# Mixing the scan's output: where the norm's scale and shift, the bonus and the mean are applied

## The chip, the core and the metric

The kernel runs on one core of a Trainium2 chip. The metric is the device time of one execution in microseconds (us). The core has a matrix engine (TensorE, "PE", with its weight loads "PEld"), three engines for elementwise work (VectorE, "DVE"; ScalarE, "ACT"; GpSimd, "POOL") and a queue that issues DMAs (SyncE, "SP"). Each engine works through its own instructions in a fixed order and waits, instruction by instruction, on what other engines have finished.

## The reference, cut to what matters

One layer of a diffusion trunk: 256 context and 1024 latent tokens of 1024 channels go through a normalised input projection, a gated convolution group and a two-direction recurrent scan (RWKV-7, eight heads of 64), an output projection with residual, and a gated MLP with a 3x3 convolution. What the change touches is the end of the scan: the sum `y` of both directions is normalised per head, scaled and shifted, a bonus is added, and the result is gated.

```python
def rwkv_output(y, r, k, v, g_lo, lp):
    mu = jnp.mean(y, axis=-1, keepdims=True)
    var = jnp.mean(jnp.square(y - mu), axis=-1, keepdims=True)
    yn = ((y - mu) * lax.rsqrt(var + GN_EPS)).reshape(bsz, t, D_RWKV) * lp["ln_g"] + lp["ln_b"]
    bonus = jnp.sum(to_heads(r) * to_heads(k) * lp["r_k"], axis=-1, keepdims=True) * to_heads(v)
    gate = jax.nn.sigmoid(g_lo) @ lp["g_up"]
    return (yn + bonus.reshape(bsz, t, D_RWKV)) * gate
```

## The kernel before

Tokens are tiled by 128, so the latents are eight tiles, t = 0 to 7. The program's stages follow one another: norm and input projection (to about 500 us of the span), decays and small inversions, the scan (about 690 to 898 us), the output side of the mixer, and the MLP: its up product (`pf`, L1105) with the 3x3 convolution, and its down product (`pf`, L1185), which fill PE from about 961 us to the end.

The scan runs in rounds, and each round takes one chunk of 64 tokens in either direction (`steps`). Its chain on PE is `ry` (L753, L761), a copy of `ry` to `rh` (L763: on ACT for one direction, on DVE for the other), `pu` (L773), a negated copy to `vu` (L777 on ACT, L779 on DVE), `ps` (L785) with the state's update on DVE (L788), and `ry` again (L794). POOL scales the chunk's `car` tile (L651) and adds up the two directions' output (L811).

From the round in which both directions have met, tiles become complete two at a time: 3 and 4, 2 and 5, 1 and 6, 0 and 7. The table `TAIL` says in which round a tile's stages are put in: `m` is `mix`, `o` is `outp` (the output projection, PE `po`, L907, 24 matmuls a tile, then DVE L1001), `h` is `to_h2` (transposes L1021 and the scaled copies L1029, L1031, L1033, L1034 that make the MLP's input). These stages are generators, and `fill` takes some steps of them between the parts of a round. Below this, a list scheduler sets the order of the instructions on every engine, so an edit in `mix` moves its neighbours too.

`mix` for one tile, by line: L965 sums `y` over each head, L966 multiplies the 8 sums by 1/64, L967 takes the mean off (all DVE); L970 squares on ACT; L972 sums the squares; `rstd_of` makes 1/sqrt(var) (L163, ACT L169, L171 to L175); L975 multiplies by it (DVE). Then POOL multiplies by the norm's scale (L976) and adds its shift (L977), and multiplies the values `vt` by the bonus factor (L978). L980 (DVE) adds `vt`, L983 (DVE) multiplies by the gate `pg` (PE, L982), L987 transposes on PE (`py`), and L989 (ACT) and L990 (DVE) split the result into the two parts `chl` that `outp` multiplies by. `mix_load` issues the DMAs of `vt` and the gate's input.

Of the kernel before, what the change touches and what calls it, by code (L numbers as in the profile page):

```python
# [11 lines left out]
ALU = mybir.AluOpType  # L12
# [75 lines left out]
def hybrid_kernel(  # L88
# [7 lines left out]
    V, A, G, PE, SY = nc.vector, nc.scalar, nc.gpsimd, nc.tensor, nc.sync  # L96
# [64 lines left out]
    def rstd_of(pool, ss, n, scale, eps):  # L161
        v = pool.tile([128, n], F32, name="rvar", bufs=2)
        V.tensor_scalar(out=v, in0=ss, scalar1=scale, scalar2=eps, op0=ALU.mult, op1=ALU.add)  # L163
        return newton(pool, v, n)
# [17 lines left out]
    bon = cp.tile([128, 8, 8], F32, name="bon")  # L182
# [23 lines left out]
    with ExitStack() as s2:  # L206
# [106 lines left out]
        while n_ < NT:  # L313
# [4 lines left out]
                               in1=prm[:, P_N1:P_N1 + 8].unsqueeze(2).to_broadcast([128, 8, 2]), op0=ALU.add, op1=ALU.mult)  # L318
# [636 lines left out]
    def mix(t):  # L955

        y, vt, sgt = mixin[t]
        xt = op.tile([128, D], F32, name="xt", bufs=XT)
        if t not in X2:
            SY.dma_start(xt, x2d[t])  # L960
        hl = op.tile([128, 2, 4, 128], F32R, name="chl", bufs=NH)
        y3 = y.rearrange("p (h n) -> p h n", n=64)
        v3 = vt.rearrange("p (h n) -> p h n", n=64)
        mu = op.tile([128, 8], F32, name="mu", bufs=2)
        V.tensor_reduce(out=mu, in_=y3, axis=mybir.AxisListType.X, op=ALU.add)  # L965
        V.tensor_scalar(out=mu, in0=mu, scalar1=1.0 / 64, scalar2=None, op0=ALU.mult)  # L966
        V.tensor_tensor(out=y3, in0=y3, in1=mu.unsqueeze(2).to_broadcast([128, 8, 64]), op=ALU.subtract)  # L967
        yield
        sq = op.tile([128, 8, 64], F32, name="ysq", bufs=2)
        A.activation(sq, y3, AF.Square)  # L970
        vr = op.tile([128, 8], F32, name="vr", bufs=2)
        V.tensor_reduce(out=vr, in_=sq, axis=mybir.AxisListType.X, op=ALU.add)  # L972
        rs = rstd_of(op, vr, 8, 1.0 / 64, epsg)
        yield
        V.tensor_tensor(out=y3, in0=y3, in1=rs.unsqueeze(2).to_broadcast([128, 8, 64]), op=ALU.mult)  # L975
        G.tensor_tensor(out=y, in0=y, in1=lng[:, 0, :], op=ALU.mult)  # L976
        G.tensor_tensor(out=y, in0=y, in1=lng[:, 1, :], op=ALU.add)  # L977
        G.tensor_tensor(out=v3, in0=v3, in1=bon[:, t, :].unsqueeze(2).to_broadcast([128, 8, 64]), op=ALU.mult)  # L978
        yield
        V.tensor_tensor(out=y, in0=y, in1=vt, op=ALU.add)  # L980
        pg = pp.tile([128, 512], F32, name="pg", tag="px", bufs=2)
        PE.matmul(pg, sgt, gup, start=True, stop=True)  # L982
        V.tensor_tensor(out=y, in0=pg, in1=y, op=ALU.mult)  # L983
        yield
        py = pp.tile([128, 4, 128], F32, name="py", tag="px", bufs=2)
        for j in range(4):
            PE.transpose(py[:, j, :], y[:, 128 * j:128 * j + 128], ident)  # L987
        yield
        A.copy(hl[:, 0], py)  # L989
        V.tensor_tensor(out=hl[:, 1], in0=py, in1=hl[:, 0].bitcast(F32), op=ALU.subtract)  # L990
        tiles[t] = [xt, hl]
# [45 lines left out]
    TPOS = {t: (0, 128 * (t - 2)) if 2 <= t < 6 else (1, 128 * (t if t < 2 else t - 4)) for t in range(8)}  # L1037

    stages = {"m": mix, "o": outp, "h": to_h2}
    ppc = Banks(ry=B2[0], pu=B2[1])  # L1040
    w_raw(0)
# [14 lines left out]
    for r in range(16):  # L1056
# [3 lines left out]
        if r == RC:  # L1060
            fill(999)
            sa.close()
            op = so.enter_context(tc.tile_pool(name="op", bufs=1, side="left", reuse_waits="tile"))
            lng = op.tile([128, 2, 512], F32, name="lng")
# [66 lines left out]
    for f in (1, 0, *range(2, NF)):  # L1131
# [24 lines left out]
        for hf, c0, n, t0 in PIECES:  # L1156
            V.tensor_tensor(out=act[:, t0:t0 + n], in0=pv[hf][:, c0:c0 + n],  # L1157
                            in1=acc.rearrange("p r c -> p (r c)")[:, t0:t0 + n], op=ALU.mult)
# [29 lines left out]
    for th in range(2):  # L1188
# [8 lines left out]
        for q in range(4):  # L1197
# [3 lines left out]
            t = 4 * th + q  # L1201
# [50 lines left out]
```

## Time and profile before

| what | value |
|---|---|
| median of 3 runs | 1689.11 us (1687.71 to 1690.62) |
| the profiled execution | 1681.7 us, its span 1679.9 us |
| mean granted TensorE clock in it | 0.949 |
| busy, share of the span | PE 91%, PEld 74%, DVE 69%, ACT 37%, POOL 34% |
| span of the mixing, from its first DVE operation to its last | 791.5 to 946.2 us |

Times in views of the trace are microseconds from the span's start. A row of the timeline gives the start, the duration, engine, line, operation and tiles of an instruction, and in brackets how long its engine had been idle before it and what ended that. A tile's name stands without its number.

### The profile page before, as it was taken

To read this page: it belongs to the slowest core of one execution; us is meant where nothing else is said; L and a number is where in the kernel's file an instruction comes from. 1 tells how busy PE (TensorE), PEld (TensorE's weight loads), DVE (VectorE), ACT (ScalarE), POOL (GpSimd) and SP (SyncE) were. 2 spreads that over 40 slices of the span, in tenths; PEclk is the share of its full clock that TensorE was granted. 3 is DMA by queue.
4 is the path that set the end of the run, shared out by engine and by line. 5 is a ranking of instruction groups with operands and counts; after the bars stand their busy time and mean duration, and the time that the engine had idled before them with its cause. 6 is when DMAs were issued, how large, how long until landed. Compare 5 with 4: busy or idle time off the path is not lost.

```text
span 1679.9 us, 27373 instructions
## 1 busy us (share of the span) xinstructions
PE 1534.4 (91%) x10567; PEld 1240.1 (74%) x10567; DVE 1154.1 (69%) x1783; ACT 619.9 (37%) x1158; POOL 567.3 (34%) x498
## 2 busy tenths in 40 slices
PE   7699999989898876898788899999999999999997
PEld 2588678767776766787666678888888887788886
DVE  5964526899899987445677678777777777346645
ACT  2654325535545235443454322221112112325323
POOL 2454413433233222412545232222222222545643
PEclk9699999989998867999899999999999999999999
DMA  9396556556665685989643112111111111533531
GB/s 322 110 290 203 173 169 189 170 164 212 209 198 167 219 261 177 335 262 278 187 133 116 51 50 62 41 49 51 50 51 51 51 40 48 190 101 124 175 93 59
DMA packets 233171, 246.93 MB, mean 147 GB/s; under 512 B 18496, under 2 KB 171685, under 8 KB 233041
## 3 DMA queue, kind: packets, MB, share of 16 engines
q1 hardware_dynamic: 232624, 245.02, 46.9%
q8 instruction: 84, 1.38, 0.4%
q14 instruction: 47, 0.38, 0.1%
q0 software_dynamic: 416, 0.16, 0.0%
HBM read 178.79 MB, written 66.33 MB: 146 GB/s over the span
## 4 chain that ended last, share of the span: by engine, by line
PE 51%; DVE 13%; ACT 2%; DMA 2%; issue 2%; POOL 1%; SPq 0%; DVEq 0%; ACTq 0%; POOLq 0%
PE pf L1105 26%; PE pf L1185 13%; PE po L907 2%; PE pco L907 2%; DVE acc L1152 2%; PE pj L355 2%; DVE ti L673 2%; PE ry L761 2%; DVE tmp L671 1%; PE ps L785 1%; PE pu L773 1%; DMA car<-ar_dram 1%; PE ry L753 1%; DVE S L788 1%; PE ry L794 1%
## 5 line engine op out<-in xcount | busy, mean ns | idle before, releaser
L1105 PE MATMUL pf<-h,fhi 128*128 128x512 f32 x1408 | 385.6, 391 | 7.6 <-DVE act L1157 4.1
L1105 PEld LDWEIGHTS pf<-h,fhi 128*128 128x128 f32 x1408 | 265.2, 189 | 64.3 <-DVE act L1157 4.5
L355 PE MATMUL pj<-hx,whi 128*128 128x512 f32 (+1 forms) x976 | 299.7, 385 | 3.0 <-DVE hx L329 1.9
L1152 DVE SCALAR_TENSOR_TENSOR acc<-gp,prm,acc 128x1024 f32<-128x1024 f32 x176 | 272.9, 1552 | 6.0
L106 POOL TENSOR_TENSOR flo<-fraw,fhi 128x1024 fp32r<-128x1024 f32 x50 | 123.2, 2465 | 305.9 <-ACT fhi L105 305.9
L1105 PE MATMUL pf<-h,flo 128*128 128x512 f32 x704 | 224.3, 391 | 0.0
L355 PEld LDWEIGHTS pj<-hx,whi 128*128 128x128 f32 x976 | 180.8, 192 | 39.6 <-issue 3.9
L355 PE MATMUL pj<-hx,wlo 128*128 128x512 f32 (+1 forms) x488 | 187.0, 383 | 0.0
L1185 PE MATMUL pf<-dhi,ahl 128*128 128x512 f32 x640 | 163.1, 389 | 0.3 <-DVE ahl L1177 0.3
L1177 DVE TENSOR_TENSOR ahl<-act,ahl 128x512 fp32r<-128x512 f32 x44 | 86.2, 1970 | 100.1 <-ACT ahl L1176 100.1
L1105 PEld LDWEIGHTS pf<-h,flo 128*128 128x128 f32 x704 | 132.7, 189 | 27.8 <-POOL flo L106 0.2
L105 ACT CAST fhi<-fraw 128x1024 fp32r<-128x1024 f32 x50 | 52.7, 1054 | 267.7 <-issue 162.5
L1185 PEld LDWEIGHTS pf<-dhi,ahl 128*128 128x128 f32 x640 | 120.0, 188 | 25.6 <-DVE ahl L1177 0.8
L106 POOL TENSOR_TENSOR dlo<-fraw,dhi 128x1024 fp32r<-128x1024 f32 x40 | 98.5, 2466 | 92.2 <-ACT dhi L105 91.4
L106 POOL TENSOR_TENSOR wlo<-wraw,whi 128x1024 fp32r<-128x1024 f32 x26 | 64.4, 2477 | 132.9 <-ACT whi L105 131.9
L1150 DVE TENSOR_SCALAR acc<-gp,prm 128x1024 f32<-128x1024 f32 x22 | 42.5, 1932 | 97.2 <-ACT gp L1142 97.2
L355 PEld LDWEIGHTS pj<-hx,wlo 128*128 128x128 f32 x488 | 93.6, 192 | 16.9 <-issue 0.8
L1185 PE MATMUL pf<-dlo,ahl 128*128 128x512 f32 x320 | 89.1, 389 | 0.0
L651 POOL TENSOR_TENSOR car<-car,pcs 128x512 f32<-128x512 f32 (+1 forms) x38 | 39.6, 1055 | 140.8 <-DMA car<-ar_dram 114.7
L105 ACT CAST dhi<-fraw 128x1024 fp32r<-128x1024 f32 x40 | 41.9, 1050 | 105.0 <-PE pf L1185 87.5
L602 PE MATMUL px<-arO,kbO 64*128 64x128 f32 (+1 forms) x640 | 65.5, 308 | 13.2 <-DVE xrO L606 8.9
L602 PEld LDWEIGHTS px<-arO,kbO 64*128 64x128 f32 x640 | 52.5, 205 | 31.4 <-issue 23.2
(292 smaller groups left out, 2620.1 us busy)
## 6 DMA issues: line engine op xcount, KB each, us to landing
araw<-in_ada_w_dram SPq DMA_DIRECT2D x48, 512.0 KB, 5.7
fraw<-in_ffn_w_up_dram SPq DMA_DIRECT2D x46, 512.0 KB, 3.9
fraw<-in_ffn_w_down_dram SPq DMA_DIRECT2D x44, 512.0 KB, 3.6
wraw<-in_w_in_dram SPq DMA_DIRECT2D x26, 512.0 KB, 4.6
lu<-lu_dram SPq DMA_DIRECT2D x20, 512.0 KB, 4.2
kb_dram<-kbT SPq DMA_DIRECT2D x40, 256.0 KB, 4.3
xa_dram<-xa SPq DMA_DIRECT2D x20, 512.0 KB, 4.4
cxa<-xa_dram SPq DMA_DIRECT2D x40, 256.0 KB, 4.2
```

Of the source, the lines that this page charges most:

```text
L105: A.copy(hi, src)
L106: G.tensor_tensor(out=lo, in0=src, in1=hi.bitcast(F32), op=ALU.subtract)
L355: PE.matmul(p[:, :n], w[:, k, :], hsl(i, k, t0, n), start=(k == 0 and first), stop=(k == 7 and last))
L602: PE.matmul(px[:, ch, i, 0:w], kbO[r, i, 2 * ch:2 * ch + 2, :].rearrange("p s n -> p (s n)"), rhs, start=True, stop=True)
L651: F3.tensor_tensor(out=self.ar, in0=self.ar, in1=self.pc.to_broadcast(list(self.ar.shape)), op=ALU.mult)
L673: V.tensor_tensor(out=ti[:, j + 1:32, 0:j], in0=ti[:, j + 1:32, 0:j], in1=tv, op=ALU.add)
L907: m = PE.matmul(po, hl[:, a_, k, :], w[k][b_][:, sl], start=(k == 0 and f), stop=(k == 3 and l))
L1105: PE.matmul(pts[hf], w[:, k, :], h2[hf][i_][:, k, :], start=(k == 0 and f), stop=(k == 7 and l))
L1150: V.tensor_scalar(out=acc, in0=src, scalar1=wcol, scalar2=prm[:, P_FB + f:P_FB + f + 1], op0=ALU.mult, op1=ALU.add)
L1152: V.scalar_tensor_tensor(out=acc, in0=src, scalar=wcol, in1=acc, op0=ALU.mult, op1=ALU.add)
L1177: V.tensor_tensor(out=hl[:, 1, :], in0=asl, in1=hl[:, 0, :].bitcast(F32), op=ALU.subtract)
L1185: PE.matmul(pd[i], hl[:, a_, 128 * q:128 * q + 128], w[w_][:, 512 * nh:512 * nh + 512], start=(f == 0 and s_), stop=(f == NF - 1 and l_))
```

## The change

The values' part is made first, at the head of `mix`: POOL multiplies `vt` by the bonus factor and adds the norm's shift to it, so both wait for the tile's DMA alone. The mean is taken off in one DVE operation, sum times -1/64 plus `y`. After the multiplication by 1/sqrt(var), DVE and no longer POOL multiplies by the norm's scale, and L980 adds `vt`, which now holds the shift. Per tile POOL has two operations where there were three, and DVE has one small one less and one of 128x512 more.

```diff
--- before.py
+++ after.py
@@ -961,10 +961,12 @@
         hl = op.tile([128, 2, 4, 128], F32R, name="chl", bufs=NH)
         y3 = y.rearrange("p (h n) -> p h n", n=64)
         v3 = vt.rearrange("p (h n) -> p h n", n=64)
+
+        G.tensor_tensor(out=v3, in0=v3, in1=bon[:, t, :].unsqueeze(2).to_broadcast([128, 8, 64]), op=ALU.mult)
+        G.tensor_tensor(out=vt, in0=vt, in1=lng[:, 1, :], op=ALU.add)
         mu = op.tile([128, 8], F32, name="mu", bufs=2)
         V.tensor_reduce(out=mu, in_=y3, axis=mybir.AxisListType.X, op=ALU.add)
-        V.tensor_scalar(out=mu, in0=mu, scalar1=1.0 / 64, scalar2=None, op0=ALU.mult)
-        V.tensor_tensor(out=y3, in0=y3, in1=mu.unsqueeze(2).to_broadcast([128, 8, 64]), op=ALU.subtract)
+        V.scalar_tensor_tensor(out=y3, in0=mu.unsqueeze(2).to_broadcast([128, 8, 64]), scalar=-1.0 / 64, in1=y3, op0=ALU.mult, op1=ALU.add)
         yield
         sq = op.tile([128, 8, 64], F32, name="ysq", bufs=2)
         A.activation(sq, y3, AF.Square)
@@ -973,9 +975,7 @@
         rs = rstd_of(op, vr, 8, 1.0 / 64, epsg)
         yield
         V.tensor_tensor(out=y3, in0=y3, in1=rs.unsqueeze(2).to_broadcast([128, 8, 64]), op=ALU.mult)
-        G.tensor_tensor(out=y, in0=y, in1=lng[:, 0, :], op=ALU.mult)
-        G.tensor_tensor(out=y, in0=y, in1=lng[:, 1, :], op=ALU.add)
-        G.tensor_tensor(out=v3, in0=v3, in1=bon[:, t, :].unsqueeze(2).to_broadcast([128, 8, 64]), op=ALU.mult)
+        V.tensor_tensor(out=y, in0=y, in1=lng[:, 0, :], op=ALU.mult)
         yield
         V.tensor_tensor(out=y, in0=y, in1=vt, op=ALU.add)
```

In the changed kernel the lines of `mix` have other numbers: L965 is now `vt` times bonus (was L978), L966 `vt` plus shift (in place of L977), L968 the sum, L969 the mean taken off, L974 the sum of squares, L977 the multiplication by 1/sqrt(var) (was L975), L978 the one by the scale (was L976, on POOL). From L980 on the numbers are the same.

The scheduler sets a new order between the first tile pair and the start of the MLP; before and behind these the order is the same. On POOL, at the first pair (tiles 3 and 4), before:

```order
L978 TENSOR_TENSOR vt<-vt,bon 128x512 x2
L651 TENSOR_TENSOR car<-car,pcs 128x512 x2
L976 TENSOR_TENSOR yt<-yt,lng 128x512
L811 TENSOR_TENSOR y<-ysum,y 64x512 x2
L977 TENSOR_TENSOR yt<-yt,lng 128x512
L976 TENSOR_TENSOR yt<-yt,lng 128x512
L651 TENSOR_TENSOR car<-car,pcs 128x512
L977 TENSOR_TENSOR yt<-yt,lng 128x512
```

And now, at the same place:

```order
L965 TENSOR_TENSOR vt<-vt,bon 128x512 x2
L966 TENSOR_TENSOR vt<-vt,lng 128x512 x2
L651 TENSOR_TENSOR car<-car,pcs 128x512 x2
L811 TENSOR_TENSOR y<-ysum,y 64x512 x2
L965 TENSOR_TENSOR vt<-vt,bon 128x512
L966 TENSOR_TENSOR vt<-vt,lng 128x512
```

No POOL operation stands any more between the multiplication by 1/sqrt(var) and the addition of `vt`; the next tile's `vt` comes in front of the next chunk's `car`.

On DVE, at the first pair, from the first tile's scaling to the copies of the scan round (`rh`, `vu`), before:

```order
L975 TENSOR_TENSOR yt<-yt,rstd_8775 128x512
L972 TENSOR_REDUCE vr<-ysq 128x8
L163 TENSOR_SCALAR rvar<-vr 128x8
L171 RECIPROCAL rstd_8833<-rstd 128x8
...
L975 TENSOR_TENSOR yt<-yt,rstd_8833 128x512
L763 COPY rh<-ry 64x512
L980 TENSOR_TENSOR yt<-yt,vt 128x512
L983 TENSOR_TENSOR yt<-pg,yt 128x512
L779 TENSOR_SCALAR vu<-pu 64x512
```

And now:

```order
L977 TENSOR_TENSOR yt<-yt,rstd_8776 128x512
L978 TENSOR_TENSOR yt<-yt,lng 128x512
L980 TENSOR_TENSOR yt<-yt,vt 128x512
L974 TENSOR_REDUCE vr<-ysq 128x8
L983 TENSOR_TENSOR yt<-pg,yt 128x512
...
L977 TENSOR_TENSOR yt<-yt,rstd_8833 128x512
L978 TENSOR_TENSOR yt<-yt,lng 128x512
L763 COPY rh<-ry 64x512
```

The first tile is finished on DVE before the second one's variance is summed, and the scan's copy `rh` stands behind more DVE work. On PE this lets the first tile's transposes (`py`) and the second's gate stand ahead of the round's `pu`, where they stood behind it.

On PE, where the output projection of the third pair (`po`, tiles 1 and 6) meets the first MLP product (`pf`), before:

```order
L907 MATMUL po<-wl_7045,chl 128x512
L907 MATMUL po<-wh_7044,chl 128x512
L1105 MATMUL pf<-h_6564,fhi 128x512
L1105 MATMUL pf<-h_6565,fhi 128x512
...
L907 MATMUL po<-wh_6919,chl 128x512
L907 MATMUL po<-wl_6920,chl 128x512
L1105 MATMUL pf<-h_6564,flo 128x512
```

And now:

```order
L907 MATMUL po<-wl_7045,chl 128x512
L907 MATMUL po<-wh_7044,chl 128x512
L1021 MATMUL ph_10040<-cst,xt 128x128 x4
L1021 MATMUL ph_10052<-cst,xt 128x128 x4
L1105 MATMUL pf<-h_6564,fhi 128x512
```

All 72 of the `pf` that come before the last pair's `py` now stand behind both tiles' `po`; 22 of them stood between the two tiles' before.

## Rows read from the trace of the kernel before

**Rows 1.** The page: engines' busy time.

```profile
PE 1534.4 (91%) x10567; PEld 1240.1 (74%) x10567; DVE 1154.1 (69%) x1783; ACT 619.9 (37%) x1158; POOL 567.3 (34%) x498
```

**Rows 2.** Stretches: window, length, busy PE, PEld, DVE, ACT, POOL; PEclk, DMA share, GB/s.

```profile
785.00:961.00 176.00, 142.33 (x1277) 112.71 (x1274) 119.59 (x235) 80.76 (x203) 75.25 (x64) 0.91 0.45 137
...
799.00:813.00 14.00, 9.04 (x90) 6.97 (x88) 10.93 (x14) 4.57 (x13) 13.74 (x11) 0.65 0.77 235
...
843.00:856.00 13.00, 10.07 (x74) 7.71 (x74) 10.13 (x17) 7.08 (x20) 9.69 (x10) 0.74 0.38 112
...
882.00:896.00 14.00, 9.06 (x148) 7.44 (x142) 11.99 (x24) 6.15 (x17) 8.59 (x7) 0.88 0.02 6
...
904.00:916.00 12.00, 10.71 (x46) 8.30 (x46) 10.35 (x19) 4.75 (x10) 4.87 (x3) 1.00 0.45 131
916.00:938.00 22.00, 16.32 (x72) 12.84 (x70) 16.38 (x28) 9.31 (x25) 13.41 (x10) 0.92 0.38 121
```

**Rows 3.** Groups by form, 785 to 961 us: busy, mean ns, idle before.

```profile
L967 DVE TENSOR_TENSOR yt<-yt,mu 128x512 f32<-128x512 f32 x2 | 1.4, 692 | 0.1
...
L966 DVE TENSOR_SCALAR mu<-mu 128x8 f32<-128x8 f32 x8 | 3.3, 428 | 0.1
...
L976 POOL TENSOR_TENSOR y<-y,lng 128x512 f32<-128x512 f32 x6 | 8.0, 1334 | 6.1 <-DVE y L975 2.3 <-DVE rstd L174 2.1 <-DVE rstd L173 1.8
L977 POOL TENSOR_TENSOR y<-y,lng 128x512 f32<-128x512 f32 x6 | 7.9, 1341 | 0.0
```

**Rows 4.** Instructions of L238: ns min/median/max.

```profile
L238 DVE SCALAR_TENSOR_TENSOR aacc<-araw,ccs,aacc x14: 729/733/752, 13.9 to 31.1; 128x512 f32<-128x512 f32 x14
```

**Rows 5.** Timeline at the first pair: start, us, instruction.

```profile
801.29 1.20 DVE L174 SCALAR_TENSOR_TENSOR rstd<-rstd,rvar 128x8 f32<-128x8 f32 x1
...
804.49 0.69 DVE L763 COPY rh<-ry 64x512 f32<-64x512 f32 x1
806.96 1.73 DVE L980 TENSOR_TENSOR yt<-yt,vt 128x512 f32<-128x512 f32 x1 [1.78 <-POOL yt L977]
...
801.20 1.28 POOL L976 TENSOR_TENSOR yt<-yt,lng 128x512 f32<-128x512 f32 x1
...
805.67 1.26 POOL L977 TENSOR_TENSOR yt<-yt,lng 128x512 f32<-128x512 f32 x1
...
805.24 1.14 PE L773 MATMUL pu<-rh,cxa 64*64 64x64 f32 x30 [1.87 <-DVE rh L763]
...
809.48 1.12 PE L987 MATMUL py<-cst,yt 128*128 128x128 f32 x4 [3.10 <-DVE yt L983]
...
813.57 0.50 PE L907 MATMUL po<-wh,chl 128*128 128x512 f32 x1
```

**Rows 6.** Timeline at the second pair.

```profile
849.90 2.76 DVE L980 TENSOR_TENSOR y<-y,vt 128x512 f32<-128x512 f32 x2 [2.62 <-POOL y L977]
...
847.63 2.77 PE L761 MATMUL ry<-S,car 128*128 128x128 f32 x12
...
853.44 1.14 PE L773 MATMUL pu<-rh,cxa 64*64 64x64 f32 x30 [1.62 <-DVE rh L763]
```

**Rows 7.** Timeline at the third pair.

```profile
889.00 1.65 DVE L975 TENSOR_TENSOR y<-y,rstd 128x512 f32<-128x512 f32 x1
...
889.18 0.32 PE L773 MATMUL pu<-rh,cxa 64*64 64x64 f32 x2 [1.77 <-ACT rh L763]
891.42 1.64 PE L773 MATMUL pu<-rh,cxa 64*64 64x64 f32 x30 [1.92 <-DVE rh L763]
```

**Rows 8.** Timeline at the fourth pair.

```profile
926.78 2.10 DVE L173 TENSOR_TENSOR rstd<-rstd 128x8 f32<-128x8 f32 x1
...
935.39 1.74 DVE L980 TENSOR_TENSOR y<-y,vt 128x512 f32<-128x512 f32 x1
...
926.08 1.97 PE L1021 MATMUL ph<-cst,xt 128*128 128x128 f32 x8 [2.29 <-DVE xt L1009]
...
937.98 0.66 PE L987 MATMUL py<-cst,y 128*128 128x128 f32 x4 [3.38 <-DVE y L983]
```

## The prediction

> **What bounds the kernel now.** I read the busy times first. PE is busy for 91% of the span [rows 1], so a change off PE pays only where PE stands and waits for what is changed. Then the table of stretches. In the 176 us from 785 to 961 us, in which all of `mix` lies, PE is busy for 142.33 us and idle for 33.7; DVE has 119.59 us of work there and POOL 75.25 [rows 2]. Inside it five windows hold most of that idle time: 4.96 us (14.00 less 9.04), 2.93, 4.94, 1.29 and 5.68, together 19.8 us [rows 2]. The granted clock is 0.65 and 0.74 of full speed in the first two, so idle time there also makes the matmuls near it slower, and 0.88, 1.00 and 0.92 in the others [rows 2].
>
> Last the timeline of these windows, to see who is late. In the first, `pu` waits 1.87 us for DVE's copy `rh`, then `py` waits 3.10 us for L983, because L980 sat behind POOL's L977 (DVE idle for 1.78 us) [rows 5]. In the second, `pu` waits 1.62 us for `rh`, which stands behind two L980 that had waited 2.62 us for POOL [rows 6]. In the third, `pu` waits 1.77 us for ACT's and 1.92 us for DVE's copy [rows 7]; the L975 ahead of DVE's took 1.65 us where 0.69 is its usual time [rows 3, 7]. In the fourth, PE waits 2.29 us for L1009 and 3.38 us for L983 [rows 8]. So the chain that ends last goes from DVE to POOL and back to DVE in two of four pairs, and through a crowded DVE in all. Behind 961 us the order does not change, and what is gained or lost ahead of it comes out at the end.
>
> **The change part by part.** POOL's work first: eight L976 go, 1.33 us each by six of them [rows 3], some 10.7 us off POOL. L977 stays in number but works on `vt`. It is off the chain: it needs the tile's `vt` and the norm's shift alone, and in the new order it stands right behind the bonus product, one to two rounds ahead of its reader. Its cover is POOL's own idle time, 100 of 176 us [rows 2]. If that cover is gone, the chunk's `car` behind it in the queue comes up to 2 x 1.34 = 2.7 us later [rows 3]; `car` is needed only in the next round. A moved pair of `vt` DMAs now stands ahead of `car` on SP and waits for the previous tile's L980, which comes sooner; I cost it at nothing and bound it by the same 2.7 us.
>
> On DVE, L966 goes: eight of 428 ns mean, 3.3 us [rows 3]. The mean's subtraction becomes a scalar_tensor_tensor. No row shows that one with a broadcast operand; the same shape with two SBUF operands takes 733 ns in L238 [rows 4], against 692 for L967 [rows 3], so +0.04 us, eight times 0.3 us; the ends are 0 and twice L967, +5.5 us in all, and I take 0.3, the row's. The scale's multiplication comes to DVE: its shape is that of L967, 0.69 us if free, 1.65 us by the stretched L975 [rows 7]; eight cost 5.5 to 13 us and I take 6.5, near the free row, since only every few such rows are stretched. So DVE gets 3.5 us more work in 176 us. What it no longer does is wait for POOL in the middle of a tile.
>
> The Trainium skill, "Vector Engine (DVE) Microarchitecture Reference", section "Points that are easy to get wrong", has a rule against this part: a scalar-tensor-tensor with two SBUF sources that are not bf16 runs at half throughput. L238 is such a case with float32 sources and shows 733 ns [rows 4], so the trace does not bear it out; by the rule the eight subtractions would cost up to 5.5 us of DVE and the gain below would shrink from 12 to about 6.5 us.
>
> Now by pair, on PE.
>
> Pair 1 (tiles 3, 4). Before: `pu` at 805.24, `py` at 809.48, the first `po` at 813.57 [rows 5]. In the new order the first tile needs, behind its L975, two free DVE operations and L983 (3 x 0.69), so its `py` and the gate run ahead of `pu`, while DVE brings `rh`. `rh` itself comes later: ahead of it stand now the first tile's scale, addition and gate and the second tile's scale, four of 0.69, less the wait for small operations that POOL had stretched (L174 took 1.20 us and ended with L976, at 802.49 and 802.48 [rows 5]). I put `pu` at 805.5 to 809.5 and `po` 1.2 us behind it; `ps`, which ran ahead of `po` before, is then still owed; it has as many matmuls as `pu`, so 1.2 us like that one's row [rows 5]. That is 807.9 to 811.9 against 813.57: a gain of 1.7 to 5.7, and I take 2.5, near the late end, as POOL is busy for 13.74 of the 14 us there [rows 2]. Lowest: -1, with every operation ahead of `rh` stretched.
>
> Pair 2 (tiles 2, 5). DVE's 2.62 us of waiting goes [rows 6], and two scales (1.4 us) come ahead of `rh`; PE's scan step ahead of it, L761, ends at 850.4, at a low clock [rows 6], and cannot be passed. From 853.44 back to that is 3 us at most; I take 2. Lowest: 0, as 2.6 less 1.4 can be eaten by one stretched operation.
>
> Pair 3 (tiles 1, 6). L976 no longer stretches L975 (1.65 - 0.69 = 0.96), one scale of 0.69 comes ahead of `rh`, and the first tile's `py` and gate run before `ps` where they ran late. What is next: `po` waits for `chl`, some 0.6 us. Of the two waits, 3.69 us [rows 7], I take 2. Lowest: 0.
>
> Pair 4 (tiles 0, 7). Both `po` of pair 3 now run back to back and all 72 `pf` behind them, so PE has some 16.6 us of work (72 x 0.23; 46 matmuls in 10.71 us at clock 1.00 [rows 2]) while DVE does the last pair, against 50 before; and DVE does scale and addition itself where it went to POOL and back, with L980 stretched to 1.74 us by L977 [rows 8]. At stake are 1.29 + 5.68 = 6.97 us [rows 2], plus about 1.5 us by which the 8 transposes at 926.08 (1.97 us) and their neighbours were slow behind the wait [rows 8]. A stall that stays: DVE behind POOL's split of MLP weights, the 2.10 us of L173 [rows 8]. What is next, then, is L1009 of the second tile and `py`; by the new DVE order L983 comes about when the 72 `pf` end. I take 5.5. Lowest: 1.5; highest 8.5.
>
> Sum: 2.5 + 2 + 2 + 5.5 = 12 us. The profiled execution of 1681.7 us would become 1669.7. That execution lies 7.4 us under the median of the runs, 1689.11; with the same 12 us off, the forecast is **1677** us. By the lowest terms (-1 + 0 + 0 + 1.5) it is 1688.6; by all the idle time, 19.8 us, 1669.3.
>
> **The rivals.** *Half of it, the last pair gains little.* The scheduler puts pair 3's two `po` side by side; if the second `chl` or the first MLP weights are late, PE waits there with no `pf` to fill in. The weights' DMA needs the scan's ring buffers, and ten of the last `ry` matmuls now stand behind the first `po`. Speaking for it: 1.29 us of PE's idle time at 904 to 916 is such a wait for weights already [rows 2]. Speaking against: the second `po` gives that DMA 24 x 0.23 = 5.6 us more. Price: pair 4 falls to 1 and pair 3 to 1; 6.5 us remain, 1682.6.
>
> *No change.* DVE, not POOL, is the engine that is late: it is busy for 10.93 of 14, 10.13 of 13 and 11.99 of 14 us in the windows where PE waits for it [rows 2], and the change gives it 3.5 us more. If each pair loses 1 us of its gain for each 0.69 added ahead of `rh` or `vu`, about ten of them, 2 us are left: 1687.
>
> *Slower: DVE stalls on POOL ahead of the scan's copies.* One mechanism: a DVE operation with two SBUF operands that meets a running POOL operation waits for its end. L174 is an operation on 8 elements, was issued when L976 ran and took 1.20 us, just to L976's end [rows 5]. The change puts more such DVE operations ahead of `rh`, and POOL's two per tile now stand together. Four more operations of 0.69 ahead of `rh` in pair 1, with about three and a half such stalls more of some 1 us, bring it 6.5 us later; `py` and the gate being done already pays most of it back, and 0.4 us are lost; with three more stalls in each later pair than I assume, each pair loses about 1.5 to 2: together +5.4 us, 1694.5. It decides from about four such stalls per pair. Against it: POOL has 10.7 us less to do. The skill, "SBUF — State Buffer", section "SBUF: two separate sides", states this as an exclusive lock that is held for the whole instruction; the trace agrees in the 1.20 us of L174 [rows 5].
>
> **How the numbers follow.** The forecast and its surroundings (gain of 8 to 18 us) get 0.50, the half 0.24, no change 0.14, slower 0.12. What a measurement of this kernel can tell from no change is about 0.2%, 3.4 us. The first two are faster by more than that, with a little of the half falling short: 0.72. Within it: 0.16. Slower: 0.12. For 8 in 10 the range goes from the full idle time, 1669, to 1690, which takes in the half, no change and the lowest terms, and leaves out most of the slower case.
>
> **What would show it.** Right: in the profile after, the scale on DVE at about 0.69 us and the subtraction at 0.73; no DVE wait for POOL ahead of L980; `py` without its 3.10 and 3.38 us of waiting; 785 to the start of the dense `pf` some 12 us shorter, with a granted clock above 0.65 and 0.74 at the first two pairs. Wrong: `rh` of the first pair later than 811 us; DVE operations of 1.2 to 2 us ahead of `rh`; PE idle before the second `po` of the third pair or before its first `pf`; the subtraction at 1.2 us or more; a stretch behind 961 us that changes its length by over 2 us.

## The result and the profile after

The changed kernel takes 1670.88 us (median of 4 runs, 1668.92 to 1673.16) against 1689.86 for the kernel before in the same session: ratio 0.9899, interval 0.9878 to 0.992. A second timing, experiment e2 below, gives 0.9917, 0.9905 to 0.993, that is 14.0 us of 1685 (11.8 to 16.0). The two intervals overlap. The forecast was 12 us and 1677.

The page of the changed kernel, engines' busy time:

```profile
PE 1532.9 (92%) x10567; PEld 1239.0 (74%) x10567; DVE 1155.0 (69%) x1783; ACT 619.7 (37%) x1158; POOL 556.3 (33%) x490
```

No engine has much less to do than in [rows 1]: POOL 11 us, DVE nothing, PE 1.5 us. What went is waiting, and matmuls that run slowly beside it. The stretches of the changed kernel, with the columns of [rows 2]; the first ends where the MLP's dense `pf` begin (960.91 before), the next five answer to the five windows of before (the third lies 2 us earlier, and the fifth is 11 us long instead of 22, since the last pair's `py` comes sooner), the last is explained below:

```profile
785.00:949.62 164.62, 137.11 (x1302) 109.19 (x1299) 119.42 (x239) 80.46 (x203) 65.03 (x58) 0.94 0.49 151
799.00:813.00 14.00, 10.01 (x94) 7.79 (x94) 11.73 (x22) 6.30 (x16) 7.52 (x7) 0.82 0.91 278
843.00:856.00 13.00, 11.24 (x114) 8.64 (x114) 11.20 (x20) 7.02 (x19) 7.23 (x8) 0.77 0.53 163
880.00:894.00 14.00, 10.61 (x144) 7.87 (x145) 13.63 (x29) 6.58 (x18) 6.14 (x5) 1.00 0.14 32
904.00:916.00 12.00, 10.86 (x51) 8.59 (x50) 11.97 (x24) 8.74 (x20) 7.17 (x5) 1.00 0.88 254
916.00:927.00 11.00, 9.79 (x47) 7.60 (x46) 10.86 (x13) 3.95 (x9) 5.97 (x4) 1.00 0.34 97
949.00:955.00 6.00, 5.38 (x16) 4.01 (x17) 1.46 (x3) 1.04 (x2) 0.00 (x0) 0.72 0.01 3
```

PE is idle for 27.5 us (164.62 less 137.11) where it was idle for 33.7, and its busy time fell from 142.33 to 137.11 us for about the same work, as the granted clock rose in four of the five windows (0.65 to 0.82, 0.74 to 0.77, 0.88 to 1.00, 0.92 to 1.00). About half of the gain is thus time in which PE was busy, at a lower clock. DVE's busy time is unchanged, 119.42 after 119.59.

Those of PE's waits in that stretch of the changed kernel that bear on the mixing (in total, times, longest); the largest of all is `ps` for the scan's `vu`, 4.0 us where it was 5.0:

```profile
PE pu L773 <- DVE rh L763: 3.9, 4, 2.2
PE py L987 <- DVE y L983: 2.3, 3, 1.2
PE ph L1021 <- DVE xt L1009: 1.7, 2, 1.5
PE pf L1105 <- ACT fhi L105: 1.1, 1, 1.1
```

`py` waited 3.10 us in the first and 3.38 in the fourth pair alone [rows 5, 8]; now all its waits together are 2.3. On DVE, what the change aims at are the waits of L980 for POOL. Before, from 785 to 961 us, they were these, and the changed kernel has none of them:

```profile
DVE y L980 <- POOL y L977: 2.6, 1, 2.6
...
DVE yt L980 <- POOL yt L977: 2.5, 2, 1.8
```

The groups by form of the changed kernel that answer to [rows 3] (L969 is the new subtraction, L978 the scale on DVE, L965 and L966 the values' part on POOL):

```profile
L969 DVE SCALAR_TENSOR_TENSOR y<-mu,y 128x512 f32<-128x512 f32 x6 | 8.2, 1358 | 0.1
L980 DVE TENSOR_TENSOR y<-y,vt 128x512 f32<-128x512 f32 x6 | 6.7, 1118 | 0.1
L978 DVE TENSOR_TENSOR y<-y,lng 128x512 f32<-128x512 f32 x6 | 4.4, 730 | 0.1
L966 POOL TENSOR_TENSOR vt<-vt,lng 128x512 f32<-128x512 f32 x8 | 10.5, 1321 | 0.3
L965 POOL TENSOR_TENSOR vt<-vt,bon 128x512 f32<-128x512 f32 x8 | 8.6, 1072 | 22.4 <-DMA vt<-v_dram 8.3 <-DVE y L978 7.0 <-DVE vu L779 6.3
```

The timeline of the changed kernel around the first pair (start, us, instruction), DVE and then PE:

```profile
799.13 0.68 DVE L969 SCALAR_TENSOR_TENSOR yt<-mu,yt 128x512 f32<-128x512 f32 x1
...
802.08 1.35 DVE L980 TENSOR_TENSOR yt<-yt,vt 128x512 f32<-128x512 f32 x1
...
808.84 0.69 DVE L763 COPY rh<-ry 64x512 f32<-64x512 f32 x1
...
800.11 0.33 PE L753 MATMUL ry<-vu,cxa 64*64 64x64 f32 x2 [3.12 <-DMA car<-ar_dram]
...
805.59 0.60 PE L987 MATMUL py<-cst,yt 128*128 128x128 f32 x4
...
809.58 0.80 PE L773 MATMUL pu<-rh,cxa 64*64 64x64 f32 x20 [2.18 <-DVE rh L763]
810.31 0.50 PE L907 MATMUL po<-wh,chl 128*128 128x512 f32 x1
```

`rh` comes at 808.84, later than the 804.49 of before, but the first tile's `py` is done before it, and `po` starts at 810.31 instead of 813.57 [rows 5]. The round itself begins 2.31 us later in this profile (800.11 for 797.80), so counted from its start `rh` comes 2.0 us later and `po` 5.6 us sooner. The third and fourth pair of the changed kernel, PE and then DVE and POOL:

```profile
886.14 0.33 PE L773 MATMUL pu<-rh,cxa 64*64 64x64 f32 x2 [1.50 <-ACT rh L763]
887.35 1.14 PE L773 MATMUL pu<-rh,cxa 64*64 64x64 f32 x30 [0.89 <-DVE rh L763]
...
926.62 0.66 PE L987 MATMUL py<-cst,y 128*128 128x128 f32 x4 [1.22 <-DVE y L983]
...
949.62 1.18 PE L1105 MATMUL pf<-h,fhi 128*128 128x512 f32 x3 [1.85 <-ACT h L1031]
...
905.57 2.86 DVE L969 SCALAR_TENSOR_TENSOR y<-mu,y 128x512 f32<-128x512 f32 x1
...
919.25 2.89 DVE L980 TENSOR_TENSOR y<-y,vt 128x512 f32<-128x512 f32 x1
...
905.52 5.17 POOL L106 TENSOR_TENSOR flo<-fraw,fhi 128x1024 fp32r<-128x1024 f32 x2 [2.85 <-ACT fhi L105]
```

`pu` waits 2.39 us for `rh` where it waited 3.69 [rows 7], `py` 1.22 where it waited 3.38 [rows 8].

To add up by place I take the *mixing stretch*: from the first `ry` of the scan round at 800.11 (797.80 before) to the dense `pf` at 949.62 (960.91). It is 149.5 us, against 163.1 before. Second profiles of the two kernels (e1, e2) give 166.9 and 149.9, so 13 to 17 us went there, 15.3 by the means. Behind it the changed kernel is slower: from 949.62 to the end it takes 721.4 and 721.1 us, before 719.0 and 719.0.

### The profile page after: what moved, and what is told of

The parts are those of the page before. It is cut to its first block, busy times and chain, and to the rows that moved or that the text cites. A ratio compares the mean times of both kernels' runs of the same rounds, so it can differ in the third digit from the quotient of the medians.

```text
span 1671.0 us, 27358 instructions
## 1 busy us (share of the span) xinstructions
PE 1532.9 (92%) x10567; PEld 1239.0 (74%) x10567; DVE 1155.0 (69%) x1783; ACT 619.7 (37%) x1158; POOL 556.3 (33%) x490
## 4 chain that ended last, share of the span: by engine, by line
PE 50%; DVE 13%; DMA 3%; ACT 2%; issue 2%; POOL 1%; SPq 0%; DVEq 0%; ACTq 0%; POOLq 0%
PE pf L1105 26%; PE pf L1185 12%; PE po L907 3%; PE pco L907 2%; DVE acc L1152 2%; PE pj L355 1%; DVE ti L673 1%; PE ry L761 1%; DVE tmp L671 1%; PE pu L773 1%; PE ps L785 1%; PE ry L753 1%; DMA car<-ar_dram 1%; PE ry L794 1%; DMA xo<-in_w_out_dram 1%
## 5 line engine op out<-in xcount | busy, mean ns | idle before, releaser
L106 POOL TENSOR_TENSOR flo<-fraw,fhi 128x1024 fp32r<-128x1024 f32 x50 | 122.2, 2444 | 313.2 <-ACT fhi L105 313.2
L1185 PE MATMUL pf<-dhi,ahl 128*128 128x512 f32 x640 | 163.1, 389 | 0.2 <-DVE ahl L1177 0.2
L106 POOL TENSOR_TENSOR dlo<-fraw,dhi 128x1024 fp32r<-128x1024 f32 x40 | 98.5, 2466 | 92.3 <-ACT dhi L105 92.3
L106 POOL TENSOR_TENSOR wlo<-wraw,whi 128x1024 fp32r<-128x1024 f32 x26 | 63.8, 2454 | 136.4 <-ACT whi L105 135.4
```

Of the source, the lines that this page charges most:

```text
L106: G.tensor_tensor(out=lo, in0=src, in1=hi.bitcast(F32), op=ALU.subtract)
L1185: PE.matmul(pd[i], hl[:, a_, 128 * q:128 * q + 128], w[w_][:, 512 * nh:512 * nh + 512], start=(f == 0 and s_), stop=(f == NF - 1 and l_))
```

## The experiments

Each was timed beside the kernel before on the same chip; four chips in all served, so runs are compared by their ratios. One profile of a kernel differs from the next of the same kernel by up to 4 us in the mixing stretch (163.1 and 166.9), so verdicts rest on the ratio, and the stretch only tells where. Its end, the *last stretch* from the first `ry` of the last scan round to the dense `pf`, is steadier: 77.2 and 78.4 us in the two profiles before, 68.1 and 69.3 in the two of the change.

| run | ratio, interval | under before, us of 1685 | mixing stretch, us |
|---|---|---|---|
| e1 before again | 0.9993, 0.9984 to 1.0002 | 1.2 | 166.9 |
| e2 the change again | 0.9917, 0.9905 to 0.993 | 14.0 | 149.9 |
| e3 one subtraction only | 1.0001, 0.9989 to 1.0013 | -0.2 | 166.0 |
| e5 values first only | 0.9964, 0.995 to 0.9977 | 6.1 | 161.7 |
| e5b scale on DVE only | 0.9984, 0.9974 to 0.9994 | 2.7 | 164.0 |
| e4 both of these | 0.995, 0.9937 to 0.9963 | 8.4 | 158.8 |
| e6 change + a DVE operation | 0.9967, 0.9952 to 0.9982 | 5.6 | 159.9 |
| e7 change + a POOL operation | 0.9921, 0.9907 to 0.9936 | 13.3 | 153.4 |
| e8 scale folded into the gate | 0.9952, 0.9934 to 0.9969 | 8.1 | 153.8 |
| e9 before, `po` ahead of `pf` | 1.0005, 0.9992 to 1.0017 | -0.8 | 166.5 |
| e10 e4, last `ry` sooner | 0.994, 0.9927 to 0.9953 | 10.1 | 158.1 |
| e12 change, order of before | 0.9934, 0.9918 to 0.995 | 11.1 | 152.2 |

**The two kernels again**, unedited, as the ground for the rest.

> The kernel before, unchanged, against itself. Both theories: ratio 1.000 within 0.002, about 1689 us. What it settles is where its profiled execution lies: that of the kernel before took 1681.7 us, 8 us under the median of its runs. If the profiled one here takes 1687 to 1692 us, the difference between two executions lies in a stage that can be named (I expect it ahead of 785 us, in stages fed by DMA, not in the mixing); if 1682 again, the profiler's execution is the faster one.

> The changed kernel again, on the same chip as the others. Theory A (the way DVE-POOL-DVE leaves the chain in each of four tile pairs): 0.990 of the kernel before, 0.988 to 0.993, and in the trace a mixing stretch 11 to 14 us shorter than before. Rival B (the 19 us of the medians are partly a matter of which chip ran): 0.993 to 0.995, as the profiled executions lie 8.5 us apart.

The kernel before equals itself (1683.6 and 1684.77 us); the change takes 1671.42, 13.35 us by the medians. The 19.0 us of the first medians lie above this interval (16.0 at most): part of them belongs to that session and not to the change.

**The parts one by one.** e3, on the kernel before:

```diff
-V.tensor_scalar(out=mu, in0=mu, scalar1=1.0 / 64, ...)
-V.tensor_tensor(out=y3, in0=y3, in1=mu..., op=ALU.subtract)
+V.scalar_tensor_tensor(out=y3, in0=mu..., scalar=-1.0 / 64, in1=y3, op0=ALU.mult, op1=ALU.add)
```

> The kernel before with only the mean's subtraction in one operation; scale, shift and bonus stay on POOL where they were. Theory A: eight small operations less on DVE, 3.3 us with what POOL stretched of them, but the way over POOL stays in the chain: 0 to 2 us faster, ratio 0.999 to 1.000. Rival C (the scheduler's new order is what pays, and any edit that makes it order anew may give or take several us): outside 0.998 to 1.002, with `po` and `pf` in another order on PE.

1684.09 us: nothing. e5 makes the values' part, bonus and shift, at the top of `mix` and leaves the scale on POOL:

```diff
+G.tensor_tensor(out=v3, in0=v3, in1=bon..., op=ALU.mult)
+G.tensor_tensor(out=vt, in0=vt, in1=lng[:, 1, :], op=ALU.add)
...
 G.tensor_tensor(out=y, in0=y, in1=lng[:, 0, :], op=ALU.mult)
-G.tensor_tensor(out=y, in0=y, in1=lng[:, 1, :], op=ALU.add)
-G.tensor_tensor(out=v3, in0=v3, in1=bon..., op=ALU.mult)
```

> The values' part with the shift first, as in the change, but the multiplication by the scale stays on POOL and the mean is taken off in two operations. The chain still goes DVE, POOL, DVE, with one POOL operation of 1.3 us per tile instead of two. Theory A: a third to a half of the gain, 5 to 9 us, ratio 0.9945 to 0.997. Rival D (what pays is that POOL is relieved of a third of its operations and stretches DVE less): 0 to 2 us, as POOL has as many operations as before. Rival C: anything from -5 to +15 us, and the order of `po` and `pf` goes with it.

1679.54 us, 6.1 less by the ratio: theory A's 5 to 9, and more than rival D allows. e5b only moves the scale:

```diff
-G.tensor_tensor(out=y, in0=y, in1=lng[:, 0, :], op=ALU.mult)
+V.tensor_tensor(out=y, in0=y, in1=lng[:, 0, :], op=ALU.mult)
```

> Only the scale's multiplication goes to DVE; shift and bonus stay on POOL where they were, two operations for the mean. The chain still crosses POOL once per tile, with one operation of 1.3 us. Theory A: like the values first alone, 3 to 7 us, ratio 0.996 to 0.998. Rival D (POOL relieved of eight operations is what pays): 8 us or more. Rival F (DVE is the bound, and 5.5 us more of work on it cost): slower by 1 to 4 us.

1683.79 us, 2.7 less: just under theory A's 3 to 7, but rival D (8 or more) and rival F (slower) both fall. `py` still waits, as in the kernel before; PE's waits from 785 to 960 us, e5b and then e5:

```profile
PE py L987 <- DVE yt L983: 4.4, 1, 4.4
```

```profile
PE py L988 <- DVE yt L984: 3.1, 1, 3.1
```

So with one POOL operation left between two of DVE the wait of the first pair stays. e4 is the change without the subtraction's edit:

> The change without its one-operation subtraction (the mean is taken off in two operations as before): values with the shift first, scale on DVE. Theory A (the way over POOL is what pays): nearly the whole gain, 11 to 14 us, ratio 0.9915 to 0.9935. Rival E (parts only pay together, the one-operation subtraction too): 6 to 9 us, as with the values first alone, which gave 5 to 6.

1678.02 us: 8.4 less, about 6.1 and 2.7 added up. That is rival E's 6 to 9; theory A's 11 to 14 failed. The subtraction's edit then goes with the rest to 14.0, 5.6 us, though by itself it is worth nothing: a difference between separate sessions, but their intervals do not meet (0.9937 and 0.993). By place the loss lies at the end: e4's last stretch takes 76.0 us, 7.3 more than the change's mean, and there e4 has another order too, as shown below.

**What an operation costs.** e6 adds to the changed kernel `V.tensor_tensor(out=y, in0=y, in1=<a column of ones>, op=ALU.mult)` behind the scale, e7 adds `G.tensor_tensor(out=vt, in0=vt, in1=<a column of ones>, op=ALU.mult)` behind the shift.

> The changed kernel with one more DVE operation per tile behind the scale's: a multiplication of 128x512 by ones, eight of about 0.69 us, 5.5 us in all. It prices a DVE operation in the chain. Theory A: four of the eight, those of the tile that is waited for, come out at the end or a little more, 2 to 4 us slower than the changed kernel, ratio 0.993 to 0.9945 to the kernel before. Rival F (DVE is the bound there): 5 us or more, ratio 0.995 and above. If nothing: DVE has slack ahead of each wait.

> The changed kernel with one POOL multiplication more per tile (vt by a column of ones, after the shift), so POOL has three wide operations per tile again, as in the kernel before, but all ahead of the tile's chain; PE's order is that of the changed kernel throughout. Theory M (what pays is that POOL is out of the chain in the middle of a tile; its load as such is hidden): within 2 us of the changed kernel, 11 to 15 us under before. Rival P (POOL's wide operations cost through the DVE operations that they hold up, wherever they stand): 10.7 us more of POOL give back 3 to 8 us, so 5 to 10 us under before, with DVE operations of 1.5 to 2 us behind L967.

Eight DVE operations of 0.69 to 0.74 us, some 5.8 us of work, cost 8.4 us (14.0 less 5.6). That is rival F's 5 or more and not theory A's 2 to 4: with POOL out of the chain, work on DVE comes out at the end in full. Eight POOL operations more, which give POOL its three wide operations per tile again, cost 0.7, less than the intervals tell apart, although PE's order is that of the changed kernel. In e7's profile the mixing stretch is 3.9 us longer than in the change's and the stretch behind is 3.8 shorter (717.6), so a cost of POOL inside the stretch is not ruled out; it does not reach the end. (Some 1.6 of the 3.8 is the clock, which falls behind 949 us in the change's profile and not in e7's; see the last section.) e6's added group, by form:

```profile
L979 DVE TENSOR_TENSOR y<-y,cst 128x512 f32<-128x512 f32 x6 | 4.4, 738 | 0.1
```

e8 takes a wide operation off DVE: `gup`, the gate's weights, is multiplied by the scale once, and `vt` by its reciprocal on POOL.

```diff
+G.tensor_tensor(out=gup, in0=gup, in1=lng[:, 0, :], op=ALU.mult)
+V.reciprocal(lng[:, 0, :], lng[:, 0, :])
...
+G.tensor_tensor(out=vt, in0=vt, in1=lng[:, 0, :], op=ALU.mult)
-V.tensor_tensor(out=y, in0=y, in1=lng[:, 0, :], op=ALU.mult)
```

> A version that may beat the changed kernel: the scale leaves the chain altogether. The gate's weights are multiplied by the scale once, and POOL multiplies the values' part by one over the scale, so that DVE has one operation of 0.69 us less per tile and POOL one of 1.3 us more, off the chain. Theory A: 2 to 4 us faster than the changed kernel, ratio 0.989 to 0.991 to the kernel before. Rival G (POOL's operations stretch DVE's two-operand ones, so what moves to POOL comes back as stalls): no gain or slower than the changed kernel, 0.992 to 0.995.

1679.77 us, slower than the change, so theory A failed. DVE's work from 785 to 959 us falls to 109.5 us, but two things outside `mix` take the gain back. The reciprocal waits for its DMA on DVE and then stands ahead of a scan's copy `rh`, so `pu` waits 7.57 us:

```profile
793.36 3.35 DVE L1070 RECIPROCAL lng<-lng 128x512 f32<-128x512 f32 x1 [7.30 <-DMA y<-y_dram]
...
797.31 1.96 PE L773 MATMUL pu<-rh,cxa 64*64 64x64 f32 x30 [7.57 <-DVE rh L763]
```

The round ahead of the first pair takes 20.3 us by this (785.41 to 805.72) where it takes 13.6 in the change; that lies ahead of the mixing stretch, and by itself it is more than e8 lost against the change (5.9 us). And PE waits 4.9 us for the MLP's first weights (`fhi`), which the change waits 1.1 us for. So e8 does not show that the fold itself fails, nor that rival G is right; a fold with its reciprocal made before the scan was not tried. The late weights led to the last question.

**Is it the chain, or PE's order?** The scheduler gives nearly every variant another order of PE in the last scan round. Ahead of the last `ry` the traces show no `po` (before, e3, e5, e6), 24 (the change, e7) or 36 (e4, e5b, e8); the expectation below counts one more. In all of these runs the first `pf` starts 6 to 8 us behind that `ry`, since the weights load into the scan's buffers. e4, first its PE, then what SP waited for ahead of a weights' DMA (L1091), then ACT:

```profile
903.23 0.33 PE L794 MATMUL ry<-vu,cxr 128*64 128x64 f32 x2
...
910.97 1.19 PE L1106 MATMUL pf<-h,fhi 128*128 128x512 f32 x2 [3.58 <-POOL h L1034]
913.47 1.22 PE L1106 MATMUL pf<-h,fhi 128*128 128x512 f32 x2 [1.30 <-ACT fhi L105]
```

```profile
SPq L1091 <- PE ry L794: 1.6, 1, 1.6
```

```profile
906.99 2.90 ACT L1030 ACTIVATE h<-ph,modc,gs 128x128 f32<-128x128 f32 x8 [1.89 <-PE ph L1022]
909.74 1.08 ACT L105 CAST fhi<-fraw 128x1024 fp32r<-128x1024 f32 x1
```

The DMA is not the whole of it. The first weights have landed at 906.99 in e4 and at 910.26 in e8, but ACT casts them to `fhi` only at 909.74 and 913.70, since `h` (L1030, in e8 L1029) stands ahead of the cast in its order; in the change the cast (904.35) follows the landing (904.28) at once and `h` comes behind it. In e4 the first wait is put down to POOL's `h`, which ended at 910.91, `fhi` at 910.82: the profile doesn't tell which of the two held PE.

e10 gives e4 at most 24 `po` ahead of the last `ry`, by the number of `mix` and `outp` steps in the slots of the last round:

```diff
-SL = (...) + ((4, 4, 4, 6),) * 5
+SL = (...) + ((4, 4, 4, 6),) * 4 + ((4, 4, 0, 10),)
```

> The change without the one-operation subtraction (that variant took 8.4 us less than before), and in the last scan round 24 po instead of 36 may stand ahead of the last ry. Theory W (the MLP's first weights can load only when the last ry has read the scan's buffers, and come 6 to 8 us later; with 37 po ahead of it they come late): last ry 3 us sooner behind the round's start, waits ahead of the first pf of 4.9 us shrink to under 2.5, 11 to 14 us under before. Theory M (the two small operations on DVE are what was missing): stays at 8 to 9 under before.

1674.73 us. The ratio goes from 0.995 to 0.994, 1.7 us, less than theory W asked for, and the intervals overlap: a gain over e4 is not shown. Its `ry` and `pf`:

```profile
896.11 0.80 PE L794 MATMUL ry<-vu,cxr 128*64 128x64 f32 x20
...
903.26 0.70 PE L1106 MATMUL pf<-h,fhi 128*128 128x512 f32 x2 [0.69 <-issue]
904.92 0.73 PE L1106 MATMUL pf<-h,fhi 128*128 128x512 f32 x2 [0.95 <-ACT fhi L105]
```

The last `ry` ends 18.8 us behind the round's start instead of 24.0, and the waits ahead of `pf` shrink from 4.9 to 2.2 us, as W has it; but then `ph` waits 2.2 us for DVE, and the last stretch is 1.1 us shorter, 74.9 us. The cast of `fhi` stands ahead of `h` on ACT there as in the change, so e10 does not separate the earlier `ry` from ACT's order. e9 takes the kernel before and holds the first `pf` behind all `po`, as they stand in the change:

```diff
+po6 = last[1]
...
-with tc.issue_after(last[1].ins) if n_ >= EI else ExitStack():
+with tc.issue_after((last[1] if n_ >= EI else po6).ins):
```

> The kernel before, with one edge more on PE: the MLP's first pf matmuls stay behind the last po of the third pair (before, 22 pf stand among that tile's po). Theory O (in the third and fourth pair it is PE's order that pays: both po together, with the MLP's weights there when they end): 5 to 9 us under the kernel before, at 1676 to 1680 where that one takes 1685, and PE's waits for xt (2.29 us) and y (3.38 us) ahead of the last pair shrink to under half. Theory M (the mixing's own chain on DVE and POOL pays): nothing in that chain is touched, so within 2 us of before.

1686.96 us: no gain. Theory O falls for the order by itself. `py` of the last pair does wait less (0.6 us), but PE's waits from 883 to 962 us show what the `pf` had filled in before:

```profile
PE po L907 <- ACT chl L989: 3.7, 2, 3.1
PE po L907 <- DVE chl L990: 3.2, 1, 3.2
```

The second tile's `chl` is late, because the chain is. The change put back into that order of before is e12 (`SL` ends in `((0, 0, 0, 18),)`, so all 48 `po` of the pair stand behind the last `ry`, and 23 `pf` among them):

> The changed kernel, arithmetic untouched; the third pair's po may only stand behind the last ry, by which the scheduler falls back to the order of before there: 23 pf among the second tile's po. Theory O: 6 to 9 us slower than the changed kernel, so only 4 to 7 us under before, with PE waits of 2 us for xt ahead of the last pair. Theory M: within 2 us of the changed kernel, 11 to 15 us under before.

1672.61 us, 13.3 less by medians, 11.1 by the ratio. PE of e12 and then its subtraction by form:

```profile
886.70 0.99 PE L794 MATMUL ry<-vu,cxr 128*64 128x64 f32 x28
...
895.81 0.73 PE L1105 MATMUL pf<-h,fhi 128*128 128x512 f32 x2 [0.89 <-ACT fhi L105]
...
915.66 1.97 PE L1021 MATMUL ph<-cst,xt 128*128 128x128 f32 x8 [2.26 <-DVE xt L1009]
...
924.96 0.66 PE L987 MATMUL py<-cst,y 128*128 128x128 f32 x4 [0.78 <-DVE y L983]
```

```profile
L969 DVE SCALAR_TENSOR_TENSOR y<-mu,y 128x512 f32<-128x512 f32 x6 | 4.0, 684 | 0.1
```

With the order of before the wait of `ph` is the one of before (2.29 us [rows 8]) and that of `py` is gone (0.78 for 3.38). The mixing stretch is 2.5 us longer than in the change and 11 to 15 us shorter than before; the last stretch, 72.1 us, is 3.4 longer and 5.7 shorter. Theory O's 4 to 7 us under before falls (8.4 by the interval's near end), and theory M holds for the greater part: 11 of the 14 us come with the order of before, and up to 3 (14.0 less 11.1) may belong to PE's order in the last round. By the times alone those 3 are not shown, as the intervals of e12 and the change overlap. Against e12, which has the same order there, e6's extra operation costs 5.5 us (11.1 less 5.6), about its work. No variant beat the change.

## Why the prediction came out

**The sum.** 12 us were forecast, 14.0 (11.8 to 16.0) were measured in e2, and the time lay within the range, 6 us under the forecast. The mixing stretch gained more, 15.3 us, and 2.2 came back behind it, which the prediction had put at nothing. The total came out nearer than its parts: every pair gave a little more than its term, and the loss behind made up for it, which was luck. Of the five signs of being wrong that it named, three came all the same: a DVE operation of over 1.2 us ahead of `rh` (1.35 at 802.08), the subtraction at over 1.2 us, and the length behind.

**Pair 1** was put at 2.5. By scan rounds (from one round's first `ry` to the next, means of two profiles) the round of pair 1 shrank from 30.2 to 26.5 us and the next, with its `po`, grew by 0.4: 3.2 us. The reason was the stated one: `py` and the gate are done ahead of a later `rh`. `pu` starts at 809.58, just behind its bracket of 805.5 to 809.5, and `po` at 810.31, inside 807.9 to 811.9; less the 2.31 us by which the round began later, both lie inside.

**Pair 2** was put at 2: its round shrank by 1.8 us, the one after it by 1.2.

**Pairs 3 and 4** were put at 2 and 5.5. The last stretch, from the round's start to the dense `pf`, went from 77.8 to 68.7 us: 9.1. The same stretch of the kernel before and of the changed one, with the columns of [rows 2]:

```profile
883.76:960.91 77.15, 63.62 (x396) 50.23 (x395) 52.92 (x104) 31.11 (x77) 31.53 (x26) 0.96 0.29 91
```

```profile
881.51:949.62 68.11, 60.29 (x395) 47.88 (x395) 52.89 (x105) 31.41 (x77) 23.66 (x20) 1.00 0.35 103
```

PE's idle time in it fell from 13.5 to 7.8 us, and its busy time by 3.3. For pair 4 the prediction put the order, both `po` together and the `pf` behind them, first, and DVE's shorter way beside it. That step was wrong in its weight: e9 has that order without the change and gains nothing, e12 has the change without it and keeps all but 2.5 us of the stretch. The order needs `chl` in time: PE's `po` waits 6.9 us for it in e9 and 0.7 in the change.

**DVE's own work** failed as a term: 3.5 us more were forecast, none were measured (119.42 after 119.59). The subtraction was costed at 0.73 us; its mean is 1358 ns over six and 1040 over the first pair's two, the first beyond the 1.2 us that was named as a sign of error. But it is not the operation that is slow: free it takes 0.68 us (799.13), and in e12 the mean of six is 684 ns. Two of the eight stand behind POOL's split of the MLP's weights, 2.86 and 2.29 us long while POOL's L106 runs from 905.52. The Trainium skill, "Vector Engine (DVE) Microarchitecture Reference", section "Points that are easy to get wrong", gives such an operation half throughput; the 684 ns beside the 692 of the plain subtraction [rows 3] do not show it. The scale's 0.69 us was right (692 and 730 ns).

**The rivals.** "No change" priced each 0.69 us of DVE ahead of the scan's copies at 1 us. e6 confirms the price (8 operations, 5.5 to 8.4 us), but not the premise: the change removed more from DVE's chain, 5.1 us of waits for POOL in the first two pairs and L966 in every tile, than it added. "Slower" was right that wide DVE operations get held up by POOL in the last pair, and wrong that this decides: most of it lies beside `pf` that PE has ready. "Half of it" named the late weights. Such a wait is real (4.9 us in e8, up to that in e4), though there it was ACT's order as much as the DMA that made them late; the changed kernel, with one tile's `po` ahead of the last `ry` and the cast ahead of `h`, is left with 1.14 us.

**What is open.** Why the subtraction's edit is worth 5.6 us on top of e4 and nothing alone. The last stretch, where e4 has another order on PE and ACT, holds most of it; how much is the order and how much L966's 3.3 us, which may count only once DVE no longer waits for POOL in the same tile, was not separated. e10 comes nearest to e4 in the change's order, but its `ph` (909.17) stands behind the first `pf` where the change's stands ahead of them (904.70), so it does not settle this.

## What to carry to other kernels

An operation on a helper engine in the middle of a chain costs more than its own time, since the chain stands in that engine's queue as well (DVE waited 5.1 us for POOL here); what depends on inputs alone belongs ahead of the chain, where even a third POOL operation per tile cost nothing measurable (e7). Judge a crowded engine by its chain and not by its busy time: DVE did the same 119 us before and after, yet one operation more per tile gave back more than half of the gain. And when a scheduler turns the order round after an edit, run the edit in the old order and the old code in the new one before crediting the order. Look, too, at where a variant's own set-up lands: e8's reciprocal made one round of the scan 6.8 us longer.

## What the runs showed of the hardware

The clock fell where it had not before. In the changed kernel PE resumes at 949.62 after a wait of 1.85 us, and from 949 to 955 us the granted clock is 0.72, between its two levels of 1.2 and 2.4 GHz, with PE busy for 5.38 of 6 us. The kernel before resumes at 960.91 after a longer wait, 2.17 us, and stays at 1.00. It is not the change that decides: of the fourteen profiles six show 0.72 there (the change, e2, e3, e5b, e6, e12, after waits of 1.81 to 1.86 us) and eight 1.00 (after 1.81 to 2.17 us), among them e7, with the change's order and a wait of 1.86 us (columns of [rows 2]):

```profile
952.21:958.21 6.00, 5.38 (x23) 4.17 (x24) 1.45 (x3) 1.04 (x2) 0.00 (x0) 1.00 0.01 3
```

Why one falls and the other doesn't stays open. In the changed kernel the next 104 recorded `pf` take 25.7 us instead of 24.0 before (25.6 in e2, 24.1 in e7): 1.7 of the 2.2 us lost behind the mixing.

A DVE operation with two operands in SBUF that met POOL's split of 2.4 to 2.9 us ended only behind it: 2.86 us at 905.57 and 2.89 at 919.25 for operations of 0.68. The time of DVE's operations above the median of their kind adds up to 20 us from 780 to 962 us in the changed kernel and 22 before (17 and 20 in the second profiles): whatever part of it is POOL's, the change moved it more than it removed it.
